# First stage of a hybrid decoder step: own buffers for every head group's raw loads, two load queues, and the squares and sums moved from GpSimd to ScalarE and VectorE

## Chip, cores and metric

One core of a Trainium2 chip. Time is the device time of one execution in microseconds; the median of several runs counts.

## What is computed

One layer of a decoder over 264 tokens (256 of a prompt, 8 of single-token samples), with 2048 features, all in float32. Cut to what matters here, and with the layer's inner branch left out:

```python
def rmsnorm(x, g):
    y = x * lax.rsqrt(jnp.mean(x * x, axis=-1, keepdims=True) + EPS)
    return y * g

hx = rmsnorm(x, norm_mix)                 # first stage: squares, sums, factors
proj = hx @ w_in                          # 2048 -> 88 tiles of 128 columns
hc, bg, cg, q, fz, iv, og, ga, gb = jnp.split(proj, cuts, axis=-1)
...                                       # short convolution branch a, HGRN2 branch o
x = x + (sigmoid(ga) * (a @ w_branch_a) + sigmoid(gb) * (o @ w_branch_b)) @ w_out
x = x + jnp.square(jax.nn.relu(rmsnorm(x, norm_ffn) @ w_up)) @ w_down
y = rmsnorm(x, norm_final)
```

## The kernel before

Features lie on the partitions, the 264 tokens on the free axis. Every operand of a product is split into a high part `hi` (rounded to float32r) and a low part `lo = x - hi`, and each product is formed as hi*hi + hi*lo + lo*hi in PSUM: three matmuls of 128x128 weights by 264 columns for each tile of 128 features (k).

**Full projection tiles** (lines 85 to 87, `gemm`): for one tile of 128 output columns a load of 1 MB (`fetch_w`, line 67) brings 16 k of weights, `split_w` (lines 58, 59) casts each half (8 k, 1024 columns) on ScalarE into `whi` and subtracts on VectorE into `wlo`, and 48 matmuls follow. All later stages have this form.

**The first stage** (lines 132 to 171) is different, since x has to arrive too. It computes the first four projection tiles (`HEAD`: q and fz of the first pair of heads) together, with k outermost: for every k it needs x of that k (`xt`, 264 columns) and the four tiles' weights of that k (`w`, 512 columns). Four groups g of four k each. Per k: cast `wh` (line 155; on VectorE for k=0, else ScalarE), `hi = x * norm` on ScalarE (line 156, `xgh`), `wl` (line 157) and `lo` (line 158, `xgl`) on VectorE, then 12 matmuls (line 162): four with (wh, hi), four with (wl, hi), four with (wh, lo). The norm's factor over the features is taken later: squares of x are formed and summed on GpSimd (lines 164 to 170) to `ss1`. After the last group three small matmuls sum `ss1` over the partitions (line 111), and the factor `rstd1` is applied to each tile as it leaves PSUM (line 445).

What orders the work: the first stage's instructions are placed by the tile framework's scheduler, which gives each engine its list at build time; an engine works its list in order and waits where an operand is missing. From line 470 on (`manual_schedule`) the program's own order holds. All loads of the first stage go out on SyncE's queue (SP): x and w in turn, line 145 and 146, and the table of parameters `pt` (line 148), which also holds the norm's weights. A raw buffer `xt` exists for each group, but the pool `wraw` of raw weights has two buffers, shared with the later `fetch_w`: the weights of group 2 wait until VectorE has made the last low part of group 0, and so on. The split weights (`wsp`) have four buffers each for hi and lo, two per group. A load also waits for the one eight loads before it to land.

Ten warm-up matmuls (line 104) keep TensorE at work while the first loads come. The zeroing of the score buffers (line 196) is GpSimd's next work after the sums.

Of the kernel before, what the change touches and what calls it, by code (L numbers as in the profile page):

```python
# [8 lines left out]
F32 = mybir.dt.float32  # L9
F32R = mybir.dt.float32r  # L10
U32 = mybir.dt.uint32
AF = mybir.ActivationFunctionType
ALU = mybir.AluOpType
AX = mybir.AxisListType

P = 128
TP = 256
TS = 8
T = TP + TS
# [19 lines left out]
@with_exitstack  # L39
def hybrid_step(ctx: ExitStack, tc: tile.TileContext, x, par, sconv, shg, w_hd, w_in, w_br, w_out, w_up, w_dn,  # L40
                y, nconv_p, nhg_p, nconv_s, nhg_s):
    """Feature-major throughout: features on partitions, the 256 prompt and 8 sample tokens on the free
    axis.  Every GEMM operand is split exactly into float32r parts (hi + lo), and each product is formed
    as hi*hi + hi*lo + lo*hi in float32 PSUM."""
    nc = tc.nc
    PS = bass.MemoryType.PSUM

# [9 lines left out]
    def split(src, hi, lo):  # L57
        nc.scalar.copy(hi, src)  # L58
        nc.vector.tensor_tensor(lo, src, hi.bitcast(F32), op=ALU.subtract)  # L59
# [8 lines left out]
        return w  # L68

    def split_w(w, h):  # L70
        """Half h of a [128, 16*128] weight chunk -> list of 8 (hi, lo) stationary tiles."""
        hi = wsp.tile([P, 8, P], F32R, tag="hi", name="whi")
        lo = wsp.tile([P, 8, P], F32R, tag="lo", name="wlo")
        split(w[:, h * 1024:(h + 1) * 1024].rearrange("p (k c) -> p k c", c=P), hi, lo)
        return [(hi[:, k], lo[:, k]) for k in range(8)]
# [13 lines left out]
    def acc_tile(name):  # L89
        return acc.tile([P, 512], F32, tag="acc", name=name)[:, :T]  # L90
# [1 line left out]
    def t264(name):  # L92
        return tmp.tile([P, T], F32, tag="t", name=name)

# [1 line left out]
    ones = const.tile([P, P], F32, name="ones")  # L96
    nc.vector.memset(ones, 1.0)
    eps = const.tile([P, 1], F32, name="eps")
# [7 lines left out]
    NB = T // 3  # L106

    def sumsq(ps, ss, start, stop):
        """Column sums of ss, tokens on partitions: ps[t, b] = sum over p of ss[p, b * NB + t]."""
        for b in range(3):  # L110
            nc.tensor.matmul(ps[:NB, b:b + 1], ss[:, b * NB:(b + 1) * NB], ones[:, 0:1],
                             start=(start and b == 0), stop=(stop and b == 2))

    def rstd_diag(ps, n, name):
        """Diagonal blocks of 1/sqrt(sum/n + eps) from the column sums in ps."""
        r = const.tile([NB, 3], F32, name="r_" + name)
        nc.vector.tensor_scalar(r, ps[:NB, 0:3], 1.0 / n, EPS, op0=ALU.mult, op1=ALU.add)
        nc.vector.reciprocal(r, r)
        nc.scalar.activation(r, r, AF.Sqrt)
        dg = const.tile([NB, 3, NB], F32, tag="dg", name="dg_" + name)  # L120
        nc.vector.tensor_tensor(dg, ident[:NB, 0:NB].unsqueeze(1).broadcast_to([NB, 3, NB]),
                                r.unsqueeze(2).broadcast_to([NB, 3, NB]), op=ALU.mult)
        return dg

    def rstd_bcast(dg, name):
        """The per-token factors of dg, on all partitions, in PSUM."""
        bps = mps.tile([P, 512], F32, tag="m", name="bps_" + name)[:, :T]
        nc.tensor.matmul(bps, ones[:NB], dg.rearrange("p b t -> p (b t)"), start=True, stop=True)
        return bps

# [1 line left out]
    pt = const.tile([P, N_PAR], F32, name="pt")  # L132
    xg = []
    ss1 = const.tile([P, T], F32, name="ss1")
# [1 line left out]
    xp = p0.enter_context(tc.tile_pool(name="xp", bufs=1))  # L136
    xsq = xp.tile([P, 4, T], F32, name="xsq")
    hps = [acc_tile(f"hd{i}") for i in range(4)]
    for g in range(4):
        xt = xp.tile([P, 4, T], F32, tag="xin", name="xt", bufs=4)  # L140
        w = wraw.tile([P, 4, 512], F32, tag="w", name="w")
        whi = [wsp.tile([P, 2, 512], F32R, tag="hi", name="whi") for _ in range(2)]
        wlo = [wsp.tile([P, 2, 512], F32R, tag="lo", name="wlo") for _ in range(2)]
        for j0, n in ((0, 1), (1, 1), (2, 2)) if g == 0 else ((0, 2), (2, 2)):
            nc.sync.dma_start(xt[:, j0:j0 + n], x[:, 4 * g + j0:4 * g + j0 + n, :])
            nc.sync.dma_start(w[:, j0:j0 + n], w_hd[g][:, j0:j0 + n])
            if g == 0 and j0 == 0:
                nc.sync.dma_start(pt, par)
        for j in range(4):
            k = 4 * g + j  # L150
            gk = pt[:, C_NMIX + k:C_NMIX + k + 1]
            hi = act.tile([P, T], F32R, tag="xg", name=f"xgh{k}")
            lo = act.tile([P, T], F32R, tag="xg", name=f"xgl{k}")
            wh, wl = whi[j // 2][:, j % 2], wlo[j // 2][:, j % 2]
            (nc.vector.tensor_copy if k == 0 else nc.scalar.copy)(wh, w[:, j])
            nc.scalar.activation(hi, xt[:, j], AF.Copy, scale=gk)
            nc.vector.tensor_tensor(wl, w[:, j], wh.bitcast(F32), op=ALU.subtract)
            nc.vector.scalar_tensor_tensor(lo, xt[:, j], gk, hi.bitcast(F32), op0=ALU.mult, op1=ALU.subtract)
            xg.append((hi, lo))
            for a, b, st, sp in ((wh, hi, k == 0, False), (wl, hi, False, False), (wh, lo, False, k == NK - 1)):  # L160
                for i in range(4):
                    nc.tensor.matmul(hps[i], a[:, i * P:(i + 1) * P], b, start=st, stop=sp)  # L162
        if g == 0:
            nc.gpsimd.tensor_tensor(xsq, xt, xt, op=ALU.mult)
        else:
            sq = xp.tile([P, 4, T], F32, tag="xsq2", name="sq", bufs=2)
            nc.gpsimd.tensor_tensor(sq, xt, xt, op=ALU.mult)
            nc.gpsimd.tensor_tensor(xsq, xsq, sq, op=ALU.add)
    nc.gpsimd.tensor_tensor(xsq[:, 0:2], xsq[:, 0:2], xsq[:, 2:4], op=ALU.add)
    nc.gpsimd.tensor_tensor(ss1, xsq[:, 0], xsq[:, 1], op=ALU.add)  # L170
    p0.close()

# [1 line left out]
    ident = const.tile([P, P], F32, name="ident")  # L174
    make_identity(nc, ident)
    cmask = const.tile([P, 2, P], F32, name="cmask")
# [5 lines left out]
    nc.gpsimd.memset(smask, 1.0)  # L182
    nc.gpsimd.memset(smask.rearrange("p a (n l) -> p (a n) l", l=CH)[:, :, 0:1], 0.0)

# [1 line left out]
    rstd1 = const.tile([P, T], F32, name="rstd1")  # L186
    ao = {}
    hctx = ExitStack()
# [15 lines left out]
        nc.gpsimd.memset(u[:, 0:2], 0.0)  # L204

    def hgrn(j, q, fz, iv, og):
        """HGRN2 of heads 2j, 2j+1, cut into stages that are issued beside successive GEMM tiles:
        stage -> (elementwise part, TensorE part)."""
        st = {}

        def s0():
# [206 lines left out]
        split(a, hi, lo)  # L418
        ao["a", c] = (hi, lo)

    # GEMM tiles in issue order, and the work to issue beside each of them
    cv = [(n, b + c, c) for c in range(NC_) for n, b in (("hc", HC), ("bg", BG), ("cg", CG))]
    seq = []
    for j in range(NH2):
# [42 lines left out]
    with tc.manual_schedule():  # L467
# [7 lines left out]
        for i in range(len(seq) + 1):  # L475
# [11 lines left out]
            if i == 0:  # L487
                gemm(ps, wk[i], xg, range(8))
                nc.scalar.copy(rstd1, rstd_bcast(dg1, "rstd1"))
                gemm(ps, wk[i], xg, range(8, 16))  # L490
                # lower bound: first entry of the softmax over the two rows of logits
                lbx = const.tile([P, 2, NC_], F32, name="lbx")
                lbm = const.tile([P, NC_], F32, name="lbm")
                lb = const.tile([P, NC_], F32, name="lb")
                oml = const.tile([P, NC_], F32, name="oml")
                lg = pt[:, C_LB:C_LB + 16].rearrange("p (r c) -> p r c", r=2)
                nc.vector.tensor_tensor(lbm, lg[:, 0], lg[:, 1], op=ALU.max)
                for r in range(2):
                    nc.vector.tensor_tensor(lbx[:, r], lg[:, r], lbm, op=ALU.subtract)
                nc.scalar.activation(lbx, lbx, AF.Exp)  # L500
                nc.vector.tensor_tensor(lbm, lbx[:, 0], lbx[:, 1], op=ALU.add)
                nc.vector.reciprocal(lbm, lbm)
                nc.vector.tensor_tensor(lb, lbx[:, 0], lbm, op=ALU.mult)
                nc.vector.tensor_scalar(oml, lb, -1.0, 1.0, op0=ALU.mult, op1=ALU.add)
            else:
                gemm(ps, wk.pop(i), xg)
# [10 lines left out]
        gemm(ps, load_w(w_in[REST.index(m)]), xg)  # L517
        nc.vector.tensor_tensor(out, ps, rstd1, op=ALU.mult)

# [1 line left out]
    mx = ctx.enter_context(tc.tile_pool(name="mx", bufs=32))  # L521
    x2p = ctx.enter_context(tc.tile_pool(name="x2p", bufs=1))
    raws.append(ctx.enter_context(tc.tile_pool(name="wraw2", bufs=2)))
# [20 lines left out]
        split(sg[0], hi, lo)  # L544
        mix.append((hi, lo))

# [1 line left out]
    x2, x2g = [], []  # L548
    ss2 = const.tile([P, T], F32, name="ss2")
    for m in range(NK):  # L550
# [18 lines left out]
        x2.append(t)  # L569
        x2g.append((hi, lo))  # L570

# [1 line left out]
    ss3 = const.tile([P, T], F32, name="ss3")  # L573
    rstd2 = None
    for qd in range(NQ):
# [36 lines left out]
                ps3 = mps.tile([P, 512], F32, tag="m", name="ps_rstd3")  # L612
                sumsq(ps3, ss3, True, False)

# [1 line left out]
    bps = rstd_bcast(rstd_diag(ps3, 2048, "rstd3"), "rstd3")  # L616
    bp = bps.unsqueeze(1)
    for m, n in ((0, 1), (1, 3), (4, 4), (8, 4), (12, 3)):
# [61 lines left out]
```

## Time and profile before

| | |
|---|---|
| runs (3) | median 1524.83 us, 1523.41 to 1525.97 |
| profiled execution, span from first to last instruction | 1522.7 us |
| TensorE (PE) busy | 1493.1 us (98%), 12182 matmul records |
| VectorE (DVE), ScalarE (ACT), GpSimd (POOL) busy | 905.4, 686.5, 128.3 us |
| first matmul of the first stage, first of the first full tile | 5.42 us, 46.10 us |

Only the span of the profiled execution is known, not its own device time; the median of the runs stands 2.1 us above that span. A busy time is the sum of an engine's instructions; matmul ends are modelled, so starts are the better guide. PEld is the load of weights into TensorE. A row of the timeline merges equal neighbours: its first number is the first start, its second the time from there to the end of the last one, "x4" their count, and in brackets stands how long the engine was idle before, and what ended that.

### The profile page before, as it was taken

The numbers are of one execution on the slowest core, as the hardware profiler recorded it, in microseconds if no ns is written. First come the engines' busy times: TensorE is split into PE (matmuls) and PEld (weight loads), VectorE is DVE, ScalarE is ACT, GpSimd is POOL, SyncE is SP. The second block draws the span as 40 slices with busy tenths as digits, with TensorE's granted clock in tenths as the row PEclk, the third lists the DMA queues.
The fourth block names the chain that finished last, engine by engine and source line by source line (L and its number), as shares of the span: only waits on it lengthen the run. The fifth ranks groups of instructions, "written<-read, shape, count | busy, mean of one in ns | idle before, by whom it ended". The sixth has DMA issues, their size and how long they took to land.

```text
span 1522.7 us, 28111 instructions
## 1 busy us (share of the span) xinstructions
PE 1493.1 (98%) x12182; PEld 1487.4 (98%) x12182; DVE 905.4 (59%) x1147; ACT 686.5 (45%) x884; POOL 128.3 (8%) x119
## 2 busy tenths in 40 slices
PE   6999999999999999999999999999999999999997
PEld 6999999999999999999999999999999999999996
DVE  8586867778655555556655544555445554455554
ACT  4454536364644444444454433444334443344452
POOL 5030404133100000001100000000000000000000
PEclk8999999999999999999999999999999999999998
DMA  5565656565655545455645454555455545454541
GB/s 191 185 238 197 250 170 249 194 250 189 236 180 181 184 176 190 171 204 194 213 167 187 174 188 173 187 173 193 168 192 172 191 169 191 169 191 170 190 166 58
DMA packets 47068, 285.90 MB, mean 188 GB/s; under 512 B 5424, under 2 KB 9024, under 8 KB 15712
## 3 DMA queue, kind: packets, MB, share of 16 engines
q1 hardware_dynamic: 46848, 283.97, 52.7%
q8 instruction: 95, 1.56, 0.4%
q14 instruction: 29, 0.24, 0.0%
q0 software_dynamic: 96, 0.14, 0.0%
HBM read 277.07 MB, written 7.02 MB: 187 GB/s over the span
## 4 chain that ended last, share of the span: by engine, by line
PE 92%; DVE 5%; DMA 1%; issue 1%; ACT 1%; SPq 0%; DVEq 0%; ACTq 0%
PE proj L85 10%; PE proj L86 9%; PE proj L87 9%; PE dn L85 8%; PE dn L87 8%; PE dn L86 8%; PE up L86 8%; PE up L85 8%; PE up L87 8%; PE wo L86 2%; PE wo L87 2%; PE wo L85 2%; DVE wlo L59 1%; PE hd L162 1%; DVE conv_a L411 1%
## 5 line engine op out<-in xcount | busy, mean ns | idle before, releaser
L58 ACT CAST whi<-w 128x1024 fp32r<-128x1024 f32 x488 | 511.1, 1050 | 766.6 <-PE dn L86 218.6
L59 DVE TENSOR_TENSOR wlo<-w,whi 128x1024 fp32r<-128x1024 f32 x488 | 604.2, 1248 | 355.5 <-ACT whi L58 353.6
L85 PE MATMUL proj<-xgh,whi 128*128 128x264 f32 x1344 | 385.3, 287 | 0.4 <-DVE q L445 0.4
L87 PE MATMUL proj<-xgh,wlo 128*128 128x264 f32 x1344 | 383.4, 285 | 0.0
L86 PE MATMUL proj<-xgl,whi 128*128 128x264 f32 x1344 | 382.6, 285 | 0.0
L85 PE MATMUL dn<-hh,whi 128*128 128x264 f32 x1024 | 293.0, 286 | 0.0
L87 PE MATMUL dn<-hh,wlo 128*128 128x264 f32 x1024 | 292.1, 285 | 0.0
L86 PE MATMUL dn<-hl,whi 128*128 128x264 f32 x1024 | 291.9, 285 | 0.0
L86 PE MATMUL up<-x2l,whi 128*128 128x264 f32 x1024 | 291.6, 285 | 0.0
L85 PE MATMUL up<-x2h,whi 128*128 128x264 f32 x1024 | 291.2, 284 | 0.0
L87 PE MATMUL up<-x2h,wlo 128*128 128x264 f32 x1024 | 290.2, 283 | 0.0
L85 PEld LDWEIGHTS proj<-xgh,whi 128*128 128x128 f32 x1344 | 254.9, 190 | 1.7 <-ACT whi L58 0.5
L86 PEld LDWEIGHTS proj<-xgl,whi 128*128 128x128 f32 x1344 | 254.7, 190 | 0.2
L87 PEld LDWEIGHTS proj<-xgh,wlo 128*128 128x128 f32 x1344 | 253.7, 189 | 0.0
L87 PEld LDWEIGHTS dn<-hh,wlo 128*128 128x128 f32 x1024 | 193.9, 189 | 0.0
L86 PEld LDWEIGHTS dn<-hl,whi 128*128 128x128 f32 x1024 | 193.7, 189 | 0.0
L87 PEld LDWEIGHTS up<-x2h,wlo 128*128 128x128 f32 x1024 | 193.7, 189 | 0.0
L85 PEld LDWEIGHTS dn<-hh,whi 128*128 128x128 f32 x1024 | 192.7, 188 | 0.0
L86 PEld LDWEIGHTS up<-x2l,whi 128*128 128x128 f32 x1024 | 192.5, 188 | 0.0
L85 PEld LDWEIGHTS up<-x2h,whi 128*128 128x128 f32 x1024 | 192.3, 188 | 0.0
L86 PE MATMUL wo<-mxl,whi 128*128 128x264 f32 x256 | 73.1, 286 | 0.0
L87 PE MATMUL wo<-mxh,wlo 128*128 128x264 f32 x256 | 73.1, 285 | 0.0
(392 smaller groups left out, 1384.1 us busy)
## 6 DMA issues: line engine op xcount, KB each, us to landing
w<-in_w_in_dram SPq DMA_DIRECT2D x84, 1024.0 KB, 4.8
w<-in_w_up_dram SPq DMA_DIRECT2D x64, 1024.0 KB, 4.7
w<-in_w_dn_dram SPq DMA_DIRECT2D x64, 1024.0 KB, 4.7
w<-in_w_br_dram SPq DMA_DIRECT2D x16, 1024.0 KB, 4.8
w<-in_w_out_dram SPq DMA_DIRECT2D x16, 1024.0 KB, 4.8
so<-in_shg_dram SPq DMA_DIRECT2D x8, 512.0 KB, 7.3
fb<-scr SPq DMA_DIRECT2D x8, 512.0 KB, 8.7
qb<-scr SPq DMA_DIRECT2D x8, 512.0 KB, 10.0
```

What stands on the lines that cost most here:

```text
L58: nc.scalar.copy(hi, src)
L59: nc.vector.tensor_tensor(lo, src, hi.bitcast(F32), op=ALU.subtract)
L85: nc.tensor.matmul(ps, wh, xh, start=(k == 0), stop=False)
L86: nc.tensor.matmul(ps, wh, xl, start=False, stop=False)
L87: nc.tensor.matmul(ps, wl, xh, start=False, stop=(k == n - 1))
L162: nc.tensor.matmul(hps[i], a[:, i * P:(i + 1) * P], b, start=st, stop=sp)
L411: nc.vector.scalar_tensor_tensor(dst, src[r], cw[r], dst, op0=ALU.mult, op1=ALU.add)
```

## The change

Each of the four groups gets raw buffers of its own for x and w (`xts`, `wts`), so no load waits for a buffer. All loads are issued ahead of the stage's loop, with high priority for the scheduler: weights on SP's queue, x of group 0 and the parameters on ScalarE's queue, x of groups 1 to 3 on SP's between the weights. For groups 1 to 3 the weights are split two k at a time (1024 columns, `split`, lines 58 and 59) instead of one. The squares go to ScalarE, their sums to VectorE. Below the core of the diff; the rest of it takes away comments.

```diff
@@ -136,41 +138,52 @@
     xp = p0.enter_context(tc.tile_pool(name="xp", bufs=1))
     xsq = xp.tile([P, 4, T], F32, name="xsq")
     hps = [acc_tile(f"hd{i}") for i in range(4)]
+    xts, wts = [], []
     for g in range(4):
-        xt = xp.tile([P, 4, T], F32, tag="xin", name="xt", bufs=4)
-        w = wraw.tile([P, 4, 512], F32, tag="w", name="w")
+        xts.append(xp.tile([P, 4, T], F32, name=f"xt{g}"))
+        wts.append(xp.tile([P, 4, 512], F32, name=f"wt{g}"))
+    with tc.high_priority():
+        nc.sync.dma_start(wts[0][:, 0:1], w_hd[0][:, 0:1])
+        nc.scalar.dma_start(xts[0][:, 0:1], x[:, 0:1, :])
+        nc.scalar.dma_start(pt, par)
+        for g in range(4):
+            for j0, n in ((1, 1), (2, 2)) if g == 0 else ((0, 2), (2, 2)):
+                nc.sync.dma_start(wts[g][:, j0:j0 + n], w_hd[g][:, j0:j0 + n])
+                (nc.scalar if g == 0 else nc.sync).dma_start(xts[g][:, j0:j0 + n], x[:, 4 * g + j0:4 * g + j0 + n, :])
+    for g in range(4):
+        xt, w = xts[g], wts[g]
         whi = [wsp.tile([P, 2, 512], F32R, tag="hi", name="whi") for _ in range(2)]
         wlo = [wsp.tile([P, 2, 512], F32R, tag="lo", name="wlo") for _ in range(2)]
-        for j0, n in ((0, 1), (1, 1), (2, 2)) if g == 0 else ((0, 2), (2, 2)):
-            nc.sync.dma_start(xt[:, j0:j0 + n], x[:, 4 * g + j0:4 * g + j0 + n, :])
-            nc.sync.dma_start(w[:, j0:j0 + n], w_hd[g][:, j0:j0 + n])
-            if g == 0 and j0 == 0:
-                nc.sync.dma_start(pt, par)
         for j in range(4):
             k = 4 * g + j
             gk = pt[:, C_NMIX + k:C_NMIX + k + 1]
             hi = act.tile([P, T], F32R, tag="xg", name=f"xgh{k}")
             lo = act.tile([P, T], F32R, tag="xg", name=f"xgl{k}")
             wh, wl = whi[j // 2][:, j % 2], wlo[j // 2][:, j % 2]
-            (nc.vector.tensor_copy if k == 0 else nc.scalar.copy)(wh, w[:, j])
-            nc.scalar.activation(hi, xt[:, j], AF.Copy, scale=gk)
-            nc.vector.tensor_tensor(wl, w[:, j], wh.bitcast(F32), op=ALU.subtract)
+            if g == 0:
+                (nc.vector.tensor_copy if k == 0 else nc.scalar.copy)(wh, w[:, j])
+                nc.scalar.activation(hi, xt[:, j], AF.Copy, scale=gk)
+                nc.vector.tensor_tensor(wl, w[:, j], wh.bitcast(F32), op=ALU.subtract)
+            else:
+                if j % 2 == 0:
+                    split(w[:, j:j + 2], whi[j // 2], wlo[j // 2])
+                nc.scalar.activation(hi, xt[:, j], AF.Copy, scale=gk)
             nc.vector.scalar_tensor_tensor(lo, xt[:, j], gk, hi.bitcast(F32), op0=ALU.mult, op1=ALU.subtract)
             xg.append((hi, lo))
             for a, b, st, sp in ((wh, hi, k == 0, False), (wl, hi, False, False), (wh, lo, False, k == NK - 1)):
                 for i in range(4):
                     nc.tensor.matmul(hps[i], a[:, i * P:(i + 1) * P], b, start=st, stop=sp)
         if g == 0:
-            nc.gpsimd.tensor_tensor(xsq, xt, xt, op=ALU.mult)
+            nc.scalar.activation(xsq, xt, AF.Square)
         else:
             sq = xp.tile([P, 4, T], F32, tag="xsq2", name="sq", bufs=2)
-            nc.gpsimd.tensor_tensor(sq, xt, xt, op=ALU.mult)
-            nc.gpsimd.tensor_tensor(xsq, xsq, sq, op=ALU.add)
-    nc.gpsimd.tensor_tensor(xsq[:, 0:2], xsq[:, 0:2], xsq[:, 2:4], op=ALU.add)
-    nc.gpsimd.tensor_tensor(ss1, xsq[:, 0], xsq[:, 1], op=ALU.add)
+            nc.scalar.activation(sq, xt, AF.Square)
+            nc.vector.tensor_tensor(xsq, xsq, sq, op=ALU.add)
+    nc.vector.tensor_tensor(xsq[:, 0:2], xsq[:, 0:2], xsq[:, 2:4], op=ALU.add)
+    nc.vector.tensor_tensor(ss1, xsq[:, 0], xsq[:, 1], op=ALU.add)
     p0.close()
```

In the changed kernel the line numbers from here on are 13 higher. TensorE's order of matmuls is the same as before in the whole kernel; on the other engines only the first stage differs. Three places in the lists of the built program follow; `xgh0` is the high part of x for k=0, `xt0` and `wt0` are the raw x and weights of group 0, and the number behind the underscore is the buffer's.

ScalarE, from its start. Before:

```order
L101 ACT_TABLE_LOAD
L101 ACTIVATE warm_82<-eps_80 128x1
L156 ACTIVATE xgh0_118<-xt_105,pt_95 128x264
L156 ACTIVATE xgh1_136<-xt_105,pt_95 128x264
L155 CAST whi_107<-w_106 128x512
L156 ACTIVATE xgh2_154<-xt_105,pt_95 128x264
L156 ACTIVATE xgh3_172<-xt_105,pt_95 128x264
L155 CAST whi_108<-w_106 128x512 x2
```

ScalarE now, from its first load to k=3:

```order
L147 DMA xt0_105<-in_x_dram 128x264
L148 DMA pt_95<-in_par_dram 128x89
L152 DMA xt0_105<-in_x_dram 128x264
L152 DMA xt0_105<-in_x_dram 128x528
L101 ACT_TABLE_LOAD
L101 ACTIVATE warm_82<-eps_80 128x1
L165 ACTIVATE xgh0_136<-xt0_105,pt_95 128x264
L164 CAST whi_132<-wt0_106 128x512
L164 CAST whi_133<-wt0_106 128x512 x2
L165 ACTIVATE xgh1_154<-xt0_105,pt_95 128x264
L58 CAST whi_209<-wt1_108 128x1024
L165 ACTIVATE xgh2_172<-xt0_105,pt_95 128x264
```

Four load issues stand ahead of the table load, and the activation of k=1 stands behind the casts of k=2 and k=3 (`whi_133`), that of k=2 behind the first cast of group 1.

VectorE at the end of the stage, ahead of the factor's first step (`r_rstd1`). Before:

```order
L157 TENSOR_TENSOR wlo_366<-w_362,whi_364 128x512 x2
L59 TENSOR_TENSOR wlo_486<-w_481,whi_485 128x1024
L59 TENSOR_TENSOR wlo_490<-w_481,whi_489 128x1024
L117 TENSOR_SCALAR r_rstd1_497<-ps1_493 88x3
```

VectorE now, where `xsq` is the running sum, `sq_431` the squares of group 3 and `wlo_474`, `wlo_478` the low parts of the first full tile:

```order
L171 SCALAR_TENSOR_TENSOR xgl12_364<-xt3_111,pt_95,xgh12_363 128x264
L181 TENSOR_TENSOR xsq_100<-xsq_100,sq_431 128x1056
L171 SCALAR_TENSOR_TENSOR xgl13_382<-xt3_111,pt_95,xgh13_381 128x264
L171 SCALAR_TENSOR_TENSOR xgl14_398<-xt3_111,pt_95,xgh14_397 128x264
L59 TENSOR_TENSOR wlo_474<-w_469,whi_473 128x1024
L171 SCALAR_TENSOR_TENSOR xgl15_416<-xt3_111,pt_95,xgh15_415 128x264
L182 TENSOR_TENSOR xsq_100<-xsq_100 128x528
L59 TENSOR_TENSOR wlo_478<-w_469,whi_477 128x1024
L183 TENSOR_TENSOR ss1_96<-xsq_100 128x264
L117 TENSOR_SCALAR r_rstd1_485<-ps1_481 88x3
```

The sums, which were GpSimd's, stand between the low parts, and `ss1` is now VectorE's last step before the factor.

SP's queue now, from its start to the first full tile:

```order
L146 DMA wt0_106<-in_w_hd_dram 128x512
L151 DMA wt0_106<-in_w_hd_dram 128x512
L151 DMA wt0_106<-in_w_hd_dram 128x1024
L151 DMA wt1_108<-in_w_hd_dram 128x1024
L152 DMA xt1_107<-in_x_dram 128x528
L151 DMA wt1_108<-in_w_hd_dram 128x1024
...
L151 DMA wt3_112<-in_w_hd_dram 128x1024
L152 DMA xt3_111<-in_x_dram 128x528
L67 DMA w_469<-in_w_in_dram 128x2048
L67 DMA w_471<-in_w_in_dram 128x2048
```

The weights of group 0 are SP's first three loads; before, x and the parameters stood between them, and the third weight load was the seventh.

## Rows read from the trace of the kernel before

**Rows 1.** The page: busy time by engine, and the chain that ended last.

```profile
PE 1493.1 (98%) x12182; PEld 1487.4 (98%) x12182; DVE 905.4 (59%) x1147; ACT 686.5 (45%) x884; POOL 128.3 (8%) x119
PE 92%; DVE 5%; DMA 1%; issue 1%; ACT 1%; SPq 0%; DVEq 0%; ACTq 0%
```

**Rows 2.** TensorE in order of time, 7 to 46 us. The row at 7.38 is the beginning of k=1.

```profile
7.38 0.71 PE L162 MATMUL hd<-xgh,whi 128*128 128x264 f32 x4
...
10.52 0.75 PE L162 MATMUL hd<-xgh,whi 128*128 128x264 f32 x4 [1.22 <-ACT whi L155]
22.71 1.25 PE L162 MATMUL hd<-xgh,wlo 128*128 128x264 f32 x4 [5.34 <-DVE wlo L157]
23.75 1.08 PE L162 MATMUL hd<-xgl,whi 128*128 128x264 f32 x4
24.64 1.08 PE L162 MATMUL hd<-xgh,whi 128*128 128x264 f32 x4
...
32.29 1.25 PE L162 MATMUL hd<-xgh,wlo 128*128 128x264 f32 x4 [4.43 <-DVE wlo L157]
45.21 0.64 PE L162 MATMUL hd<-xgl,whi 128*128 128x264 f32 x4
45.69 0.56 PE L111 MATMUL ps<-ones,ss 128*88 128x1 f32 x6
46.10 0.37 PE L85 MATMUL proj<-xgh,whi 128*128 128x264 f32 x1
```

**Rows 3.** Stretches of 1 us: length, busy time of each engine, then the granted clock of TensorE, the share of the DMA engines and GB/s.

```profile
20.00:21.00 1.00, 0.00 (x0) 0.00 (x0) 1.00 (x2) 1.00 (x3) 1.00 (x2) 0.51 0.00 0
26.00:27.00 1.00, 1.00 (x7) 1.00 (x7) 1.00 (x1) 0.00 (x0) 1.00 (x1) 0.58 0.33 98
30.00:31.00 1.00, 0.00 (x0) 0.00 (x0) 1.00 (x3) 0.91 (x3) 0.14 (x1) 0.62 0.03 12
37.00:38.00 1.00, 1.00 (x10) 1.00 (x9) 0.27 (x1) 0.00 (x0) 0.00 (x0) 0.96 1.03 434
```

**Rows 4.** Waits up to 50 us: who waited for whom, total us, times, longest. The last row is SP's queue.

```profile
ACT whi L155 <- DMA w<-in_w_hd_dram: 11.4, 5, 8.1
PE hd L162 <- DVE wlo L157: 9.8, 2, 5.3
SPq L146 <- DVE wlo L157: 12.4, 2, 11.2
```

**Rows 5.** First the stretch that holds all of GpSimd's sums (columns as in rows 3), then one of them, then VectorE, in order of time.

```profile
7.00:31.00 24.00, 14.30 (x93) 13.15 (x91) 23.52 (x18) 13.17 (x28) 18.87 (x9) 0.84 0.60 217
...
15.12 2.79 POOL L168 TENSOR_TENSOR xsq<-xsq,sq 128x1056 f32<-128x1056 f32 x1
...
5.34 0.89 DVE L158 SCALAR_TENSOR_TENSOR xgl<-xt,pt,xgh 128x264 fp32r<-128x264 f32 x2
15.52 4.79 DVE L158 SCALAR_TENSOR_TENSOR xgl<-xt,pt,xgh 128x264 fp32r<-128x264 f32 x2
20.23 5.27 DVE L157 TENSOR_TENSOR wlo<-w,whi 128x512 fp32r<-128x512 f32 x2
34.38 0.48 DVE L158 SCALAR_TENSOR_TENSOR xgl<-xt,pt,xgh 128x264 fp32r<-128x264 f32 x1
```

**Rows 6.** Durations of one instruction. First two rows with count, min/median/max in ns; the others are groups by form with count, busy us, mean ns.

```profile
L158 DVE SCALAR_TENSOR_TENSOR xgl<-xt,pt,xgh x16: 478/487/2692, 5.3 to 34.4; 128x264 fp32r<-128x264 f32 x16
L157 DVE TENSOR_TENSOR wlo<-w,whi x16: 675/681/2918, 4.7 to 36.6; 128x512 fp32r<-128x512 f32 x16
...
L158 DVE SCALAR_TENSOR_TENSOR xgl<-xt,pt,xgh 128x264 fp32r<-128x264 f32 x16 | 16.1, 1049 | 0.2 <-ACT xgh L156 0.2
L157 DVE TENSOR_TENSOR wlo<-w,whi 128x512 fp32r<-128x512 f32 x16 | 16.0, 1040 | 1.1 <-ACT whi L155 1.1
L59 DVE TENSOR_TENSOR wlo<-w,whi 128x1024 fp32r<-128x1024 f32 x488 | 604.2, 1248 | 355.5 <-ACT whi L58 353.6
L620 DVE TENSOR_TENSOR x2t<-x2t,bps_rstd 128x1056 f32<-128x1056 f32 x2 | 2.4, 1249 | 0.0
L216 DVE TENSOR_TENSOR q<-q,sig 128x528 f32<-128x528 f32 x4 | 2.8, 710 | 5.0 <-ACT sig L214 5.0
L58 ACT CAST whi<-w 128x1024 fp32r<-128x1024 f32 x488 | 511.1, 1050 | 766.6 <-PE dn L86 218.6 <-PE up L86 187.7 <-PE proj L86 165.7
L155 ACT CAST whi<-w 128x512 fp32r<-128x512 f32 x15 | 8.6, 615 | 11.6 <-DMA w<-in_w_hd_dram 11.4
```

**Rows 7.** ScalarE's first two activations, and SP's issue of the third weight load, in order of time; then what landed of the issues from 3.6 to 3.7 us (this load alone): count, KB, us from issue to landing.

```profile
4.64 0.92 ACT L156 ACTIVATE xgh<-xt,pt 128x264 fp32r<-128x264 f32 x2 [2.33 <-DMA pt<-in_par_dram]
3.62 0.43 SPq L146 DMA_DIRECT2D w<-in_w_hd_dram  x1
...
w<-in_w_hd_dram SPq DMA_DIRECT2D x1, 512.0 KB, 6.2
```

**Rows 8.** Stretches of 4 us, columns as in rows 3.

```profile
0.00:4.00 4.00, 2.87 (x13) 2.87 (x14) 0.17 (x2) 1.49 (x2) 2.02 (x11) 1.00 0.44 128
4.00:8.00 4.00, 4.00 (x25) 3.88 (x23) 2.61 (x5) 1.92 (x4) 0.23 (x1) 1.00 0.84 256
8.00:12.00 4.00, 2.78 (x19) 2.32 (x19) 3.84 (x6) 2.61 (x7) 1.81 (x1) 1.00 1.00 335
12.00:16.00 4.00, 4.00 (x35) 4.00 (x35) 4.00 (x5) 3.56 (x8) 2.92 (x2) 1.00 1.03 401
```

## The prediction

> **What bounds the kernel now.** I read the page first: TensorE (PE) is busy for 98% of the span and holds 92% of the chain that ended last, while GpSimd (POOL) is busy for 8% [rows 1]. The kernel is one long TensorE stream, and a change at its start is worth as much as it lets the stream start sooner. I mark the start by the first matmul of the first full projection tile, at 46.10 us [rows 2].
>
> PE's order of time from there backwards shows what the first stage costs [rows 2]. Its 192 matmuls (16 k, 12 each) take 0.121 us each where nothing stops them (four from 45.21 to 45.69). Behind the warm-up matmuls k=0 ends and k=1 begins at 7.4; 7.4 + 180 x 0.1213 = 29.2 would be the end of k=15, and it is 45.7. Missing are 16.5 us: waits of 1.2, 5.3 and 4.4 us, matmuls at half rate behind the two long ones (four from 23.75 to 24.64, 0.22 us each), and small waits. The granted clock says why: it falls from 1.00 to 0.50 near 20.0 and near 30.2 (waits begun at 17.4 and 27.9, so 2.6 and 2.4 us into them), and is back near 26.8 and 37.1, that is 4.1 and 4.8 us after PE resumed [rows 3]. These are its two levels, 2.4 and 1.2 GHz. The wait of 1.2 us before 10.5 cost no clock: four matmuls behind it took 0.75 us.
>
> Who holds PE: the low parts on VectorE (DVE) [rows 4]. DVE and POOL side by side [rows 5]: while POOL squares and adds, two low parts of 264 columns take 4.79 us (from 15.5) and two of 512 take 5.27 (from 20.2); at 5.3, before POOL's first square, two of 264 take 0.89, and at 34.4, after its last sum, one takes 0.48. By form, the same instruction runs from 0.48 to 2.69 us and from 0.68 to 2.92 [rows 6]. POOL's whole work is thus paid by DVE. Second holder: the loads. SP's own queue waited 12.4 us for DVE before a weight load (it needs one of two raw buffers back), and the casts of ScalarE (ACT) waited 11.4 us for weights [rows 4].
>
> **Part by part.**
> *POOL's work goes.* Four squares, three adds, two folds leave POOL, 18.9 us [rows 5]. DVE's excess goes with it: 16.1 us of low parts of x where 16 x 0.487 = 7.8 would do, 16.0 of low parts of weights where 16 x 0.68 = 10.9 would do, 13.4 us in all [rows 6].
>
> *Squares on ACT, sums on DVE.* No row has a square of 1056 columns; it is nearest to ACT's cast of 1024, 1.05 us, so 1.08 [rows 6], between 1.05 and the 1.25 of DVE's final scaling of 1056. Four are 4.3 us. An add of 1056 on DVE I take at those 1.25, between two subtractions of 512 (1.36) and 1.2; a fold of 528 at 0.71, of 264 at 0.48 [rows 6]: 3 x 1.25 + 1.19 = 4.9 us. Beside PE's 21.8 us these matter only if ACT or DVE ends last, which is summed below.
>
> *Splits of 1024.* From group 1 on, two casts of 512 become one of 1024: 1.05 for 2 x 0.615, and 1.22 for 2 x 0.68 on DVE [rows 6]. A gain of 0.15 us per half group on either, off PE's path.
>
> *Loads.* ACT issues four; at SP's 0.43 each and the gaps between [rows 7] its table load slips by 1.9 us. That costs nothing: before, ACT stood idle for 2.3 us until the parameters landed, at 4.64 [rows 7]. On SP, the weights of group 0 are out by 2.2 us, not 4.0, and no load waits for a raw buffer any more; the first two full projection tiles follow at once. At 335 to 401 GB/s [rows 8] all of the 8.4 MB lands by 25 to 28 us, each piece before its cast.
>
> *The new wait, which decides.* ACT's order now puts the casts of k=2 and k=3 **ahead of** the activation of k=1 (the order rows above), so k=1 waits for the third weight load, which it did not need before. When does it land? Before: issued at 3.62, landed 6.2 us later, at 9.8 [rows 7]. Until then the engines moved 0.51 + 1.02 + 1.8 x 0.335 = 2.1 MB [rows 8], 0.5 MB of it loads queued behind. With issue no longer the limit I let them move 0.6 MB by 4.0 and 0.32 MB per us after: the 1.64 MB of group 0 alone are in at 7.3, with 0.5 MB of others between them at 8.8. I take 8.2, since later loads again stand right behind. The Trainium skill speaks against more (DMA: Bandwidth & Descriptors, section "Issuing engines are not separate DMA queues"): loads issued by two engines run on the same 16 DMA engines, and only issue time is saved. By it the sum stays as it is; if a second queue brought bandwidth of its own, the early rival below would hold, 1510.2. No run here shows two load queues at once.
>
> Then: 8.2 + 0.62 + 0.53 (two casts) + 0.50 (activation) + 0.05 = 9.9 for the first matmul of k=1 [rows 6, 7]. PE has finished k=0 at 7.4: idle 2.5 us, as long as it took the clock to fall in both rows, so an even matter. I let it fall, because every tenth of a microsecond by which the load is later speaks for it, and return 4.4 us after PE resumes: in these, 20 matmuls run where 36 would, a loss of 2.0 us.
>
> **The sum.** 9.9 + 180 x 0.1213 (21.8) + 2.0 = 33.7 for the end of k=15. Neighbours on ACT and DVE overlap a little (two activations take 0.92 us [rows 7]), so from start to start: ACT, from 9.9: 14 activations at 0.41, 8 casts at 1.0, 4 squares at 1.06 = 18.0, so 28 us: ahead. DVE, from 10.1 (8.2, two casts, the low part of k=3): 15 low parts at 0.42, 8 of 1024 at 1.15, the sums 4.9 = 20.4, with about 1 us of waits for ACT 31.5: ahead of 33.7, so the sum of squares, now last on DVE, is covered by 2 us. (If the clock does not fall, PE would end at 31.7 or a little later, DVE at 31.5: the cover is gone, and some 0.3 us may be paid.) The three column-sum matmuls take 0.41 us as now [rows 2]: the projection starts at 34.1 instead of 46.1, **12.0 us sooner**. PE's order and every other engine's are the same from there on, and PE has no wait there that hangs on the start: 1522.7 - 12.0 = 1510.7 for the span. The median of the runs stands 2.1 us above the profiled span, so 1512.8.
>
> **Rivals.**
> *Loads early.* The third load lands by 7.3: idle 7.3 + 1.7 - 7.4 = 1.6 us, and the clock stays. End 9.0 + 21.8 + 0.3 = 31.1, start 31.5, gain 14.6: 1510.2. For: the 8 to 12 us stretch ran at 335 GB/s with full engines. Against: before 8 us the rate was 256 [rows 8]. If the clock stays at my own landing time, 2.0 us less and 0.3 more make 1511.1. Together 0.33.
>
> *Loads late.* Small loads on ACT's queue share the engines and the third weight load lands at 9.8 as before, or a microsecond later. Then 9.8 + 1.7 + 21.8 + 2.0 = 35.3, start 35.7, gain 10.4: 1514.4; 1515.4 with the extra microsecond. Chance 0.20.
>
> *DVE stays slow.* If the stretched DVE work came from load traffic and not from POOL, DVE's 31.5 becomes 44.9 and the gain is 0.8: 1524.0. Against: between 20 and 21 us, where nothing is loaded [rows 3], it was just as stretched, and at 5.3 under 256 GB/s it was not [rows 5, 8]. Chance 0.03.
>
> *Clock never back: slower.* Short waits for operands that come just in time hold the clock at 0.50 through the stage: 9.9 + 180 x 0.22 = 49.5, start 49.9, 3.8 us later than now: 1528.6. Each matmul at half rate loses 0.1 us, and 13.9 us are to be lost: it decides from about 140 matmuls on. For: ACT delivers k=2 to k=5 hardly faster than PE uses them. Against: after both long waits the clock came back, to the full rate of rows 2 [rows 2, 3]. The Trainium skill tells of such a kernel (TensorE: Matmul & The Clock Gate, section "HAM oscillation — how this bites in real kernels"), where each burst starts cold after a wait. Chance 0.03.
>
> **The numbers.** Forecast 1512.8, chance 0.40; early or clock kept 0.33; late 0.20; the last two 0.03 each; 0.01 for a faster case not listed. The range takes in early and late with about 0.7 us for the scatter of a median: 1509.5 to 1516.3. What can be told from no change is 0.2%, 3 us. Faster 0.94, same 0.03, slower 0.03.
>
> **What would show it.** Right: POOL empty from 3 us to the zeroing of its score buffers; no low part of 264 columns above 0.6 us; a single long PE wait, 2 to 3 us before k=1, ended by ACT's activation, with clock 0.50 behind it; projection near 34. Wrong: PE waits on DVE in groups 2 and 3, a wait for the sum of squares above 1 us, or clock 0.50 beyond 16 us.

## The result, and the profile after

The median of four runs is 1511.16 us (1507.88 to 1516.3) against 1524.67 us (1523.41 to 1525.97, four runs): ratio 0.9916, 95% interval 0.9894 to 0.9938, 13.5 us or 0.9% faster. The profiled execution is the slowest of the four, 1516.3 us with a span of 1514.6, so its lines explain the stage, and not the median.

The page after, busy time by engine, answers to the first of [rows 1]:

```profile
PE 1491.6 (98%) x12182; PEld 1485.9 (98%) x12182; DVE 895.9 (59%) x1146; ACT 689.6 (46%) x882; POOL 109.6 (7%) x110
```

POOL lost 18.7 us, and DVE 9.5, although DVE took over five instructions. TensorE in order of time, the part that answers to [rows 2]:

```profile
6.10 1.06 PE L175 MATMUL hd<-xgh,whi 128*128 128x264 f32 x4 [0.34 <-ACT xgh L165]
...
8.68 0.75 PE L175 MATMUL hd<-xgh,whi 128*128 128x264 f32 x4 [0.55 <-ACT xgh L165]
...
12.17 0.75 PE L175 MATMUL hd<-xgh,whi 128*128 128x264 f32 x4 [1.78 <-ACT xgh L165]
...
14.29 1.08 PE L175 MATMUL hd<-xgh,whi 128*128 128x264 f32 x4
...
17.48 0.64 PE L175 MATMUL hd<-xgh,wlo 128*128 128x264 f32 x4
...
34.43 0.56 PE L111 MATMUL ps<-ones,ss 128*88 128x1 f32 x6
34.85 0.37 PE L85 MATMUL proj<-xgh,whi 128*128 128x264 f32 x1
```

The first full tile begins at 34.85 us instead of 46.10, 11.25 sooner. The two waits of 5.3 and 4.4 us on VectorE are gone; three for ScalarE's activations stand in the stage now (0.34, 0.55 and 1.78 us), 2.67 us in all. Four matmuls take 0.65 us at the full rate and 1.08 behind the longest wait. The stretches of 1 us (columns as in [rows 3]) show why:

```profile
13.00:14.00 1.00, 0.98 (x7) 0.77 (x6) 0.83 (x3) 1.00 (x4) 0.00 (x0) 0.82 1.04 417
14.00:15.00 1.00, 1.00 (x7) 1.00 (x6) 0.56 (x3) 1.00 (x2) 0.00 (x0) 0.50 1.02 411
...
17.00:18.00 1.00, 1.00 (x10) 1.00 (x10) 1.00 (x3) 1.00 (x3) 0.00 (x0) 0.97 1.07 419
```

By the means of these stretches the clock falls to its lower level, 1.2 GHz, near 13.6, 1.5 us after the wait has ended, and is back at 2.4 GHz near 17.1. VectorE's low parts, ns of the shortest, median and longest (for [rows 6]), and GpSimd's first work after its masks:

```profile
L171 DVE SCALAR_TENSOR_TENSOR xgl<-xt,pt,xgh x16: 486/495/502, 6.1 to 29.2; 128x264 fp32r<-128x264 f32 x16
...
31.94 0.56 POOL L209 MEMSET scm<- 128x256 f32 x2 [29.27 <-DVE ss L183]
```

The longest low part was 2692 ns and is 502. ScalarE in order of time shows what the three waits hang on (for [rows 7]); then what landed of four issues, from 1.24, 1.7 and 2.2 us on (count, KB, us to landing):

```profile
1.24 0.45 ACTq L148 DMA_DIRECT2D pt<-in_par_dram  x1
...
5.54 0.52 ACT L165 ACTIVATE xgh<-xt,pt 128x264 fp32r<-128x264 f32 x1 [1.34 <-DMA pt<-in_par_dram]
...
7.07 1.14 ACT L164 CAST whi<-wt 128x512 fp32r<-128x512 f32 x2 [0.50 <-DMA wt<-in_w_hd_dram]
8.12 0.51 ACT L165 ACTIVATE xgh<-xt,pt 128x264 fp32r<-128x264 f32 x1
10.66 1.04 ACT L58 CAST whi<-wt 128x1024 fp32r<-128x1024 f32 x1 [2.03 <-DMA wt<-in_w_hd_dram]
11.61 0.51 ACT L165 ACTIVATE xgh<-xt,pt 128x264 fp32r<-128x264 f32 x1
12.02 1.07 ACT L177 ACTIVATE xsq<-xt 128x1056 f32<-128x1056 f32 x1
```

```profile
pt<-in_par_dram ACTq DMA_DIRECT2D x1, 44.5 KB, 4.2
...
wt<-in_w_hd_dram SPq DMA_DIRECT2D x1, 512.0 KB, 5.3
...
wt<-in_w_hd_dram SPq DMA_DIRECT2D x1, 512.0 KB, 8.4
xt<-in_x_dram ACTq DMA_DIRECT2D x1, 264.0 KB, 8.6
```

The third weight load landed at 7.05 us, the parameters only at 5.45, the first weights of group 1 at 10.65 and x of k=2 and 3 at 10.8. The activation of k=2 stands behind the cast of group 1's weights.

Of the 11.25 us, 8.1 are left at the end of this execution's span. Between the stage and the last full tiles the clock is at half for 10.2 us in sum (summed over stretches of 1 us) where it was for 6.8 before, by half of the difference 1.7 us of loss more; the waits for `kend` in the later stages are 4.0 us where they were 3.0; and the part behind the last matmul is 0.7 us longer.

### The profile page after: what moved, and what is told of

Its sections match the earlier page's. It is cut to its first block, busy times and chain, and to the rows that moved or that the text cites. A ratio compares the mean times of both kernels' runs of the same rounds, so it can differ in the third digit from the quotient of the medians.

```text
span 1514.6 us, 28096 instructions
## 1 busy us (share of the span) xinstructions
PE 1491.6 (98%) x12182; PEld 1485.9 (98%) x12182; DVE 895.9 (59%) x1146; ACT 689.6 (46%) x882; POOL 109.6 (7%) x110
## 4 chain that ended last, share of the span: by engine, by line
PE 93%; DVE 4%; DMA 1%; ACT 1%; issue 0%; SPq 0%; DVEq 0%; ACTq 0%
PE proj L85 9%; PE proj L86 9%; PE proj L87 9%; PE dn L85 8%; PE dn L87 8%; PE up L85 8%; PE dn L86 8%; PE up L86 8%; PE up L87 8%; PE wo L86 2%; PE wo L87 2%; PE wo L85 2%; DVE wlo L59 2%; PE hd L175 1%; DMA w<-in_w_in_dram 1%; DVE conv_a L424 1%
```

## The experiments

All ran in three or five rounds beside the kernel before. "Start" is the first matmul of the first full tile in the run's profile (46.10 before, 34.85 after).

| run | start | median us (range) | ratio, 95% interval |
|---|---|---|---|
| e0 changed kernel again | 32.58 | 1511.25 (1510.47 to 1513.11) | 0.9922 (0.9907 to 0.9936) |
| e1 squares and sums alone | 33.21 | 1512.22 (1511.57 to 1513.70) | 0.9928 (0.9913 to 0.9942) |
| e2 buffers and loads alone | 44.04 | 1524.63 (1522.46 to 1526.07) | 1.0006 (0.9996 to 1.0015) |
| e3 one load queue | 32.58 | 1510.47 (1508.51 to 1511.91) | 0.9914 (0.9899 to 0.9929) |
| e4 e3 and idle products on GpSimd | 39.23 | 1517.20 (1515.77 to 1520.52) | 0.9960 (0.9946 to 0.9974) |
| e5 order by hand | 33.06 | 1511.72 (1510.12 to 1513.17) | 0.9925 (0.9908 to 0.9941) |
| e6 finer loads and splits | 32.07 | 1511.92 (1510.03 to 1512.21) | 0.9920 (0.9906 to 0.9935) |
| e7 e3 and idle memsets on GpSimd | 32.16 | 1510.12 (1508.93 to 1512.33) | 0.9913 (0.9898 to 0.9928) |
| e8 later products on VectorE | 31.98 | 1503.53 (1502.57 to 1505.72) | 0.9867 (0.9852 to 0.9881) |
| e9 e8 and 1 - fb on ScalarE | 33.35 | 1501.43 (1500.93 to 1502.57) | 0.9852 (0.9837 to 0.9867) |
| e10 e3 again | 32.07 | 1509.24 (1508.50 to 1512.23) | 0.9909 (0.9892 to 0.9925) |

**e0_after_again**: no edit.

> The changed kernel once more, unchanged. In its first profile the first full projection tile began at 34.85 us (46.10 before), but 3 us of that lead were lost later, where TensorE's granted clock fell at 105.9 and at 266 us behind waits of 0.8 to 2.6 us. Theory A (the clock's fall behind such short waits is chance, from execution to execution): the projection starts at 33 to 35 again, but the later stretches at clock 0.50 lie elsewhere or are missing, and the runs spread over several us (1506 to 1516). Theory B (the change itself moved those later waits so that the clock falls): the same two stretches again, at 106 and 266 us, and runs close to 1514.

```profile
11.40 0.75 PE L175 MATMUL hd<-xgh,whi 128*128 128x264 f32 x4 [0.99 <-ACT xgh L165]
32.58 0.37 PE L85 MATMUL proj<-xgh,whi 128*128 128x264 f32 x1
...
14.00:15.00 1.00, 1.00 (x11) 1.00 (x10) 0.90 (x1) 1.00 (x3) 0.00 (x0) 1.00 1.03 417
```

The same program, and its three waits are 0.45, 0.53 and 0.99 us; k=2 begins at 11.40, and the stretches of 12 to 17 us stand at clock 1.00. The falls at 106 and 266 us are missing, and one of 6.8 us begins at 167, so theory A holds in the main and theory B does not: where the clock falls differs between executions of one program. From k=2 to the first full tile it takes 21.18 us, and 22.68 in the first profile: the fall cost 1.5 us there, the later start of k=2 0.77.

**e1_sums_only**: the kernel before, with the squares and sums moved and nothing else; two of the five changed lines:

```diff
...
-            nc.gpsimd.tensor_tensor(sq, xt, xt, op=ALU.mult)
-            nc.gpsimd.tensor_tensor(xsq, xsq, sq, op=ALU.add)
+            nc.scalar.activation(sq, xt, AF.Square)
+            nc.vector.tensor_tensor(xsq, xsq, sq, op=ALU.add)
...
```

> The kernel before, with the squares on ScalarE and the sums on VectorE, and nothing else: two raw weight buffers, loads on SP's queue in the old order. Theory P (GpSimd's work was the loss, and the buffers' waits followed from VectorE's lateness): group 2's weights are issued at about 11.8 and group 3's near 16.5 instead of 25, projection start 31.5 to 34.0, total 1509 to 1513. Theory L (early loads from buffers of their own are needed as well): TensorE still waits for groups 2 and 3, several us each, projection start 38 to 42, total 1517 to 1521.

**e2_loads_only**: the changed kernel with these five lines put back to GpSimd.

> The changed kernel with squares and sums back on GpSimd: own buffers, early loads, two queues, wide splits. Theory P: VectorE's low parts are stretched again whenever GpSimd works (264 columns up to 2.7 us), TensorE waits for them, projection start 38 to 42, total 1517 to 1521. Theory L: with operands loaded early VectorE has slack to absorb the stretching, projection start 34 to 36, total 1511 to 1514.

The two halves do not share the gain. e1 has nearly all of it, within the ranges of its theory P. e2 starts 2.1 us sooner than the kernel before, later than either of its theories said, and its total can't be told from that kernel's. TensorE's waits in e1, then e2's longer ones; e2's low parts; and VectorE and GpSimd in e2, in order of time:

```profile
10.42 0.75 PE L162 MATMUL hd<-xgh,whi 128*128 128x264 f32 x4 [1.47 <-ACT whi L155]
21.47 0.76 PE L162 MATMUL hd<-xgh,wlo 128*128 128x264 f32 x4 [1.18 <-DVE wlo L157]
```

```profile
15.68 1.25 PE L175 MATMUL hd<-xgl,whi 128*128 128x264 f32 x4 [2.76 <-DVE xgl L171]
25.84 0.76 PE L175 MATMUL hd<-xgh,wlo 128*128 128x264 f32 x4 [1.63 <-DVE wlo L59]
28.41 1.11 PE L175 MATMUL hd<-xgl,whi 128*128 128x264 f32 x4 [1.80 <-DVE xgl L171]
...
L171 DVE SCALAR_TENSOR_TENSOR xgl<-xt,pt,xgh x16: 479/484/2672, 5.9 to 37.7; 128x264 fp32r<-128x264 f32 x16
...
13.45 9.45 DVE L171 SCALAR_TENSOR_TENSOR xgl<-xt,pt,xgh 128x264 fp32r<-128x264 f32 x4
...
15.41 2.50 POOL L181 TENSOR_TENSOR xsq<-xsq,sq 128x1056 f32<-128x1056 f32 x1
```

With every load out early, four low parts still take 9.45 us, 2.36 us each, beside GpSimd instructions of 2.1 to 2.5 us. In e1 the loads still wait for raw buffers, but VectorE gives these back sooner: SP's queue waits 5.4 us for them, 3.5 at the longest, where it waited 12.4 and 11.2 [rows 4], and TensorE waits for none of these loads after k=2. The long wait of SP's queue was a consequence of the late low parts, not a cause of its own.

**e3_one_queue**: the changed kernel, x ahead of the weights and the parameters third, all on SP's queue.

```diff
+        nc.sync.dma_start(xts[0][:, 0:1], x[:, 0:1, :])
...
-        nc.scalar.dma_start(xts[0][:, 0:1], x[:, 0:1, :])
-        nc.scalar.dma_start(pt, par)
+        nc.sync.dma_start(pt, par)
...
+                nc.sync.dma_start(xts[g][:, j0:j0 + n], ...)
...
-                (nc.scalar if g == 0 else nc.sync).dma_start(xts[g][:, j0:j0 + n], ...)
```

> The changed kernel with all first-stage loads on SP's queue, x ahead of the weights of the same k, parameters third, as in the kernel before; own buffers and sums as in the change. The scheduler then places the activation of k=1 ahead of the casts. Theory Q (the second queue costs: its x loads and the parameters land late, since both queues share the engines, and what each needs first is not first): k=0 at 5.4 instead of 6.1, one wait of 1 to 2 us before k=2, projection start 31 to 33, total 1508 to 1511. Theory R (the second queue helps, it saves issue time): k=2 starts later than 12.2 and the projection later than 34.9.

```profile
4.68 0.52 ACT L165 ACTIVATE xgh<-xt,pt 128x264 fp32r<-128x264 f32 x1 [2.37 <-DMA pt<-in_par_dram]
...
9.24 0.50 ACT L165 ACTIVATE xgh<-xt,pt 128x264 fp32r<-128x264 f32 x1
9.68 1.14 ACT L164 CAST whi<-wt 128x512 fp32r<-128x512 f32 x2
```

In ScalarE's list the parameters are there 0.9 us sooner than with two queues, and k=0 begins at 5.42. TensorE waits 1.07 us before k=2, as theory Q has it. But the start is that of e0, which has two queues, and the totals can't be told apart: that the second queue costs is not shown either. It brought nothing here. The Trainium skill (DMA: Bandwidth & Descriptors, "Issuing engines are not separate DMA queues") says that loads issued by several engines run on the same 16 DMA engines and that only issue time is saved; the runs agree, with ratios of 0.9914 on one queue and 0.9922 on two.

**e4_junk_pool** and **e7_junk_memset**: e3 with GpSimd work on a buffer that nobody reads, seven products in e4, sixteen memsets in e7.

```diff
+    for _ in range(7):
+        nc.gpsimd.tensor_tensor(junk2, junk, junk, op=ALU.mult)
```

```diff
+    for _ in range(16):
+        nc.gpsimd.memset(junk2, 1.0)
```

> The one-queue kernel (projection start 32.6 us, GpSimd empty in the stage) with seven products of 1056 columns on GpSimd, from a scratch tile into another, which nothing else reads or waits for; they start at once and last some 15 us or more. Theory P1 (GpSimd's two-operand work itself stretches VectorE's, whatever tiles it touches): VectorE's low parts beside it take up to 2.7 us again, TensorE waits for VectorE between 7 and 20 us, projection start 38 to 42, total 1516 to 1520. Theory P2 (the stretch came from sharing x's tiles or from waits between the two engines): low parts stay under 0.7 us, projection start 32 to 33.5, total 1508 to 1512.

> As the kernel with seven idle products, but with sixteen memsets of 1056 columns on GpSimd in their place, which write a scratch tile and read nothing. Theory M1 (any GpSimd work stretches VectorE): stretched low parts and a projection start of 36 us or later. Theory M2 (only GpSimd work that reads operands does): low parts under 0.7 us, projection start 32 to 33.5.

The low parts and GpSimd's longest run in e4, and then in e7:

```profile
L176 DVE SCALAR_TENSOR_TENSOR xgl<-xt,pt,xgh x16: 476/479/2174, 5.6 to 34.2; 128x264 fp32r<-128x264 f32 x16
L171 DVE TENSOR_TENSOR wlo<-wt,whi x4: 691/2428/2430, 5.0 to 17.1; 128x512 fp32r<-128x512 f32 x4
...
8.11 10.88 POOL L157 TENSOR_TENSOR junk<-junk 128x1056 f32<-128x1056 f32 x5
```

```profile
L176 DVE SCALAR_TENSOR_TENSOR xgl<-xt,pt,xgh x16: 480/486/632, 5.5 to 27.2; 128x264 fp32r<-128x264 f32 x16
L171 DVE TENSOR_TENSOR wlo<-wt,whi x4: 682/692/693, 4.9 to 11.5; 128x512 fp32r<-128x512 f32 x4
...
6.92 13.46 POOL L157 MEMSET junk<- 128x1056 f32 x13
```

No data passes between the engines, and the products alone cost 6.7 us of start and, by the two ratios, 7 us of time, while memsets as dense cost nothing. So P1 and M2 hold: GpSimd work that reads its operands stretches VectorE's, whatever tiles it touches. Two limits: the products differ from the memsets in their arithmetic too, which these two runs do not separate from the reading; and in e4 the one cast of VectorE beside a product, a step with one input, took 0.86 us (0.43 in e7). The 632 ns in e7 ran beside a mask's select on GpSimd, which reads; beside a memset the next low part took 0.48 us. The Trainium skill (SBUF — State Buffer, "🔬 SBUF: two separate sides") says that the two engines share ports which one instruction holds to its end, and that VectorE's steps with two SBUF inputs meet this only against a GpSimd step that reads SBUF; both runs agree, 2174 against 632 ns.

**e5_by_hand**: the changed kernel's stage in an order written by hand, each activation behind its own cast, squares and sums two k later.

```diff
+    with tc.manual_schedule():
+        for g in range(4):
...
+                if j == 2 and g > 0:
+                    sums(g - 1)
```

> The changed kernel with the first stage in a fixed order: on ScalarE each k's activation right behind its cast, so that k=1 does not wait behind the casts of k=2 and k=3, nor k=2 behind the cast of group 1; the squares of a group behind the first half of the next. Two queues as in the change. Theory O (ScalarE's order made the waits before k=1 and k=2): k=1 at 7.9, k=2 at 8.5 to 9.5, projection start 30.5 to 32. Theory D (x of k=2 and 3, last on ScalarE's queue, lands at 10.3 to 10.8 and would hold k=2 anyhow): k=1 at 7.9, k=2 at 11.0 to 11.5 after one wait of 1.5 to 2 us, projection start 31.5 to 32.5, or 2 us more if the clock falls behind that wait.

Start 33.06. The wait before k=2 was 1.19 us, since its x, last on ScalarE's queue, landed at 10.57: as theory D has it, the landing of x, not the order of ScalarE's list alone, holds k=2. A wait of 0.82 us for the sum of squares came in, VectorE's last step, which neither theory had. The total can't be told from e0's.

**e6_fine**: e3 with a load for each k in group 0, and group 1 split one k at a time.

```diff
-            for j0, n in ((1, 1), (2, 2)) if g == 0 else ((0, 2), (2, 2)):
+            for j0, n in ((1, 1), (2, 1), (3, 1)) if g == 0 else ((0, 2), (2, 2)):
...
-            if g == 0:
+            if g < 2:
```

> The one-queue kernel with the loads of k=2 and k=3 issued one by one, and narrow splits (512 columns) in group 1 as well. Theory: its waits of 1.07 us (k=2, for weights of two k in one load) and 0.50 us (k=4, for a wide low part) shrink to under 0.4 us together: projection start 31.0 to 31.6, total 1507 to 1510, the fastest so far. Rival: every further load costs 0.47 us of issue on the one queue and pushes all later ones back: k=4 then waits 0.5 to 1 us, projection start 32.3 to 33, no gain over the one-queue kernel.

Start 32.07, later than the theory said: 0.96 us of wait are left before k=2 and 0.31 at 17.5 us, where under 0.4 in sum was expected. The total can't be told from e3's. What is left of the stage's waits is too small to show.

**e8_products_dve**, **e9_products_and_fb**, **e10_one_queue_again**: what e4 showed, used on the later stages of e3.

```diff
-            nc.gpsimd.tensor_tensor(so, so, fb, op=ALU.mult)
+            nc.vector.tensor_tensor(so, so, fb, op=ALU.mult)
...
-            nc.gpsimd.tensor_tensor(qb, qb, so, op=ALU.mult)
+            nc.vector.tensor_tensor(qb, qb, so, op=ALU.mult)
...
-        nc.gpsimd.tensor_tensor(u[:, 2:], cg[:, :TP], hc[:, :TP], op=ALU.mult)
+        nc.vector.tensor_tensor(u[:, 2:], cg[:, :TP], hc[:, :TP], op=ALU.mult)
...
```

```diff
-            nc.gpsimd.tensor_scalar(fb, fb, -1.0, 1.0, op0=ALU.mult, op1=ALU.add)
+            nc.scalar.activation(fb, fb, AF.Copy, scale=-1.0, bias=1.0)
```

> The kernel with one load queue, and in the later stages the four kinds of two-operand products of GpSimd (L267 and L278, 128x1024, eight each; L410 and L411, eight each) formed on VectorE at the same place of its list. Theory (GpSimd's two-operand work stretches VectorE's wherever they meet): the waits for VectorE at 101 (1.0 + 0.3 us), 167 (2.6) and 261 us (1.8 + 0.3) shrink to 0.5 us or less each, since the multiplication of kend and kk takes 0.68 us everywhere (now 2.82 once) and the conv_a step 0.5 (now up to 1.5); the two later falls of the clock go with them. Gain 3 to 6 us of waits and 3 us of clock, less than 1 us of new waits: 1502 to 1506 against 1510.5. Rival: VectorE carries 8 x 1.25 + 8 x 1.25 + 8 x 0.5 = 24 us more and falls further behind at the same places: waits as long or longer, 1510 to 1515.

> As the run before, and the step 1 - fb (L268, 128x1024, eight of 1.1 to 1.9 us on GpSimd) on ScalarE. Theory: L268 reads one operand from memory and still overlaps conv_a's steps and low parts; away from GpSimd it leaves VectorE undisturbed there: 0 to 1.5 us sooner than the run before. Rival: ScalarE reaches the step before the product is done and holds the casts behind it: new waits for whi of 0.5 us or more, 0 to 4 us later than the run before.

> The one-queue kernel unchanged, as the measure for the two others of this call: 1510.5 us, between 1508.5 and 1512.5; the stage as before, first full tile at 32.6; falls of the clock behind none, one or two of the waits at 101, 167 and 261 us, 6.8 us at half rate in sum the last time.

Busy time by engine, TensorE's wait for `kend`, and VectorE's two kinds of step that had been stretched, in e10; then the same lines of e8, and the second kind in e9:

```profile
PE 1487.5 (99%) x12182; PEld 1482.3 (98%) x12182; DVE 897.2 (60%) x1146; ACT 689.7 (46%) x882; POOL 108.2 (7%) x110
...
168.40 0.33 PE L312 MATMUL trps<-ident,kend 128*128 128x128 f32 x1 [2.53 <-DVE kend L300]
...
L300 DVE TENSOR_TENSOR kend<-kend,kk x4: 680/684/2826, 83.9 to 322.3; 128x512 f32<-128x512 f32 x4
L424 DVE SCALAR_TENSOR_TENSOR conv_a<-ub,pt,conv_a x16: 477/485/2510, 87.9 to 381.2; 128x256 f32<-128x256 f32 x16
```

```profile
PE 1485.1 (99%) x12182; PEld 1480.1 (99%) x12182; DVE 896.3 (60%) x1178; ACT 690.4 (46%) x882; POOL 45.5 (3%) x78
...
L300 DVE TENSOR_TENSOR kend<-kend,kk x4: 685/685/686, 82.6 to 315.0; 128x512 f32<-128x512 f32 x4
L424 DVE SCALAR_TENSOR_TENSOR conv_a<-ub,pt,conv_a x16: 476/484/1142, 85.5 to 375.9; 128x256 f32<-128x256 f32 x16
```

```profile
L424 DVE SCALAR_TENSOR_TENSOR conv_a<-ub,pt,conv_a x16: 478/485/486, 88.5 to 374.9; 128x256 f32<-128x256 f32 x16
```

VectorE does 32 instructions more in e8 and is busy 0.9 us less: the work came at no charge. The waits at 101 and 168 us are gone, that at 254 is 1.23 us, more than the 0.5 expected (0.39 in e9), and between the stage and the tail no stretch of e8 or e9 shows a clock below full. The rival, VectorE falling further behind, is refuted. Not separated is what it brings that the products, 2.5 us each on GpSimd, are also done sooner. e8 and e9 are the fastest of all, 5.7 and 7.8 us below e10. e9 is 2.1 us below e8, past the 1.5 expected; their intervals overlap. One such place is left in every run, the sums of the second norm (L581). In e9:

```profile
L575 DVE SCALAR_TENSOR_TENSOR x2l<-x2t,pt,x2h x16: 482/988/996, 653.1 to 740.8; 128x264 fp32r<-128x264 f32 x16
...
658.57 0.99 POOL L581 TENSOR_TENSOR ss<-ss,sq 128x264 f32<-128x264 f32 x1 [6.51 <-ACT sq L580]
```

Fifteen of sixteen low parts take 0.98 to 1.00 us beside GpSimd's fifteen sums instead of 0.48, and no wait of TensorE stands there: the stretch costs time only where TensorE waits for it.

## Why the prediction was right, and where it was off

- **GpSimd's work is paid by VectorE**: right, and nearly all of the gain. e1 has it alone, e4 brings it back with work that has no reader.
- **Second holder, the loads**: wrong as a cause of its own. e2 keeps every early load and gains nothing that can be told. What its rows showed was VectorE's lateness seen from the queue.
- **Durations**: the square, put at 1.08, took 1.07 us, and VectorE kept ahead: its last step for `ss1` ended at 31.83, and the column sums began at 34.43 without a wait.
- **"The new wait, which decides"**: of the right size in sum, 2.67 us for 2.5, but in the wrong place, and that the two agree is luck. The third weight load was put at 8.2 us and landed at 7.05, so k=1 waited 0.55. Group 1's first weights, not priced on the path, landed at 10.65, and k=2 waited 1.78 for the activation behind their cast. The fall of the clock then came behind k=2 and not behind k=1. From k=2 the sum is 12.17 + 168 x 0.1213 = 32.55, and the rest up to 34.43, 1.9 us, is mostly the clock's, put at 2.0.
- **"That costs nothing"**, of ScalarE's issues: off by 0.7 us at k=0, 6.10 for 5.42; it did not reach k=2, which waited for group 1's weights. The parameters left sooner but landed 0.9 us later than on one queue.
- **The clock**: called even and let fall. It fell in the first profile and not in e0, the same program. The 2.4 us and more into a wait that it took in the kernel before was no bound: behind 1.78 us it fell once. One sign of being wrong came true in the first profile, clock 0.50 beyond 16 us: it was back near 17.1, not at 14.3. In e0 the start is 32.58, 1.1 us from the early rival's 31.5 and 1.5 from the forecast's 34.1. The median, 1511.16, is 1.6 below the forecast and lies on the rival in which the clock stays (1511.1). That the first profile's start, 34.85, is so near 34.1 rests on a fall of the clock that did not come again in e0.
- **"PE has no wait there that hangs on the start"**: not quite. The later waits stay, but whether the clock falls behind them differs from one execution to the next: 10.2, 6.8 and 3.4 us at half rate after the stage in the first profile, e0 and e10. The mean granted clock of the four runs fits this: 0.992 in the slowest and 0.997 in the fastest, by an estimate (0.005 of 1510 us) 7.5 of the 8.4 us between them. The waits differ a little too, those for `kend` 4.0 us in the first profile and 3.0 in e0.

Still open is what decides, for a wait of 1 to 3 us, whether the clock falls.

## What to carry to other kernels

Before sharing elementwise work out to an idle GpSimd, look at one VectorE instruction's shortest and longest time: where a 0.5 us step takes 2.5 beside a GpSimd step, moving the GpSimd work onto the busier VectorE can be free. It pays only where TensorE waits for the stretched step. A wait for a buffer in a load queue is a cause only if its release would be late anyway; undo it alone to see. A second load queue brought nothing here: with the DMA engines 0.9 busy and more from 2 us on, the parameters were issued sooner and landed later, so look at when the first pieces land, not at when they are issued.

## What the runs showed of the hardware

- Beside GpSimd work that reads memory, VectorE's two-input steps last about as long as GpSimd's instruction: 2.43 us beside products of 2.18 (e4), 0.99 beside sums of 1.00 (e9). A one-input GpSimd step of 1.22 us does it too: 1142 ns at worst in e8, 486 in e9 without it. Beside memsets as dense the low parts stay at 0.48 to 0.49 us (e7).
- From the end of the wait for `kend` near 170 us to the next wait TensorE's stream takes 90.4 us in e1 and e10, where the clock stays, 91.8 in the first profile with a stretch of 3.4 us at half rate, and 93.1 in e0 and the kernel before with one of 6.8: a fall costs 1.4 or 2.7 us there. Behind equal waits it comes in one execution and not in the next: after 3.02 us at 168 us in e0 it fell, after 3.03 us at 170 us in e1 it did not.
- Loads on two queues at once: 44.5 KB took 4.2 us to land and 264 KB 8.6, beside 512 KB loads of the other queue that took 5.3 to 8.4. On one queue in the order of need (e3) the same two loads took 2.9 and 4.7.
